# Moving the block-causal mask of the prompt attention from separate products into extra rows of its score products

## The chip, the cores and the metric

The kernel runs on one core of one Trainium2 chip. The metric is the device time of one execution in microseconds (us). Before the change the median of three executions is 3446.71 us (3445.31 to 3451.4).

## The reference

One inference step of a one-layer hybrid streaming encoder, in float32. What matters here is group A, attention with 8 heads over 2064 rows of a prompt (16 meta rows and 2048 frames) in chunks of 64 frames. A frame sees the meta rows and every frame of its own and of earlier chunks:

```python
chunk_p = jnp.where(frame_p < 0, -1, frame_p // CHUNK)          # CHUNK = 64

def attend(q, k, v, mask):
    s = jnp.einsum('bqhd,bkhd->bhqk', q, k).astype(jnp.float32) * (QK_HEAD ** -0.5)
    if mask is not None:
        s = jnp.where(mask, s, -jnp.inf)
    p = jax.nn.softmax(s, axis=-1).astype(v.dtype)
    return jnp.einsum('bhqk,bkhd->bqhd', p, v)

    # per block of queries: attend(q_blk, k, v, c_blk[:, None] >= chunk_id[None, :])
```

Queries and keys have 96 entries a head (64 without position, 32 with rotary position). Input projection, a gated delta rule (group B), the attention of 64 new rows over a cache, output projection and MLP are the rest of the work. The change leaves them alone.

## The kernel before

**Stages.** The program runs an input projection (0 to about 545 us), a gated delta rule with the queries' projection beside it (to about 975 us), the prompt's attention (about 977 to 1715 us), the attention of the new rows (to about 1810 us) and output projection with MLP (to the end). float32 products are taken as three products of a high and a low part.

**Attention.** A job is a head and a block of 512 queries: 4 pairs of heads, 2 heads, 4 blocks, 32 jobs in all, in an order written out in `HB0`. Keys lie in 17 tiles, mostly of 128, in 4 chunks that end where a block of 512 queries does. Three kinds of work are interleaved on the engines.

- `kv_chunk` works out keys and values of two heads for a chunk. The key tile `kn` holds rows of 97 numbers: 96 entries and a constant 1 in column 96, set by GpSimd (L866). TensorE transposes it (L913), and ScalarE and VectorE split it into the high part `KTh` and the low part `KTl`, with the key's entries in rows 0 to 96.
- `prep` makes a job ready. It loads the queries (L938, on SP's queue), and `q_head` transposes them (L925) and splits them into `qh` (L928, ScalarE) and `ql` (L929, VectorE). Then it finds the greatest score of each query: for each of the four groups of 128 queries a product over all keys that these see, in pieces of up to 512 keys (L952), and a maximum over each piece by VectorE (L955). On the last piece of each group a product with one row of contraction (L954) adds -1e30 to the last 64 keys for the first 64 queries. The four maxima a partition are transposed (L960), negated (L962) and sent by a DMA on SP's queue into row 96 of `qh` (L963), so that the product with the keys' constant 1 subtracts the maximum.
- `main_block` takes the transposed scores of a key tile as three products (L983, L984, L986) into PSUM, ScalarE takes their exponential (L990), ScalarE and VectorE split this in two (L133, L134), and four steps of work later three products with the values follow (L1003, L1004, L1005). The four key tiles that reach the diagonal get a fourth score product with two rows of contraction (L988), which adds -1e30 where a query does not see a key:

```python
edge = i > 4 * b
nc.tensor.matmul(ps[:w, off:], kl[:96, s:s + w], qh[:96, off:], start=False, stop=not edge)
if edge:
    nc.tensor.matmul(ps[:w, off:off + 128], self.negk[:, :w], self.negk[:, 128:], start=False, stop=True)
```

That makes 4 x 32 = 128 products on L954 and 128 on L988. Their operands are small constants that `attn_open` builds with VectorE.

**Order.** `attention` issues the units of the main blocks in order and, between them, as many steps of the two streams of side work (keys, preparation) as their deadlines call for; a preparation may begin three jobs ahead of its main block. Each engine and each DMA queue executes its list in a fixed order. `qh` and `ql` rotate over 4 buffers (`QB`), so the queries of job n take the buffer of job n-4. PSUM holds 2 score tiles, 3 tiles of the maxima's products, 1 of the results and 2 for the rest.

Of the kernel before, what the change touches and what calls it, by code (L numbers as in the profile page):

```python
# [22 lines left out]
T = LP + DEC  # L23
# [9 lines left out]
# columns of the transposed activations: new sample rows, meta rows, frames  # L33
# [29 lines left out]
# order of the output projection's products: group of columns, half of it, half of the rows  # L63
# [3 lines left out]
KVW, QW = 4, 8  # L67
PB, HB, SSB, QB = 5, 4, 2, 4
# [12 lines left out]
# key tiles of the prompt, in chunks that end where a block of 512 queries does  # L81
# [11 lines left out]
def key_chunk(c):  # L93
    """first column, columns and tiles of a chunk."""
    t = TILES[tile_index(c):4 * c + 5]
    return t[0][0], t[-1][0] + t[-1][1] - t[0][0], t


def prepass_cuts(b, i):
    """the keys that 128 queries see, in pieces (chunk, from, to)."""  # L100
    r = []
    for c in range(b + 1):
        s0, n, _ = key_chunk(c)
        n = min(n, 144 + 128 * (4 * b + i) - s0)
        k = -(-n // 512)
        r += [(c, n * j // k, n * (j + 1) // k) for j in range(k)]
    return r
# [10 lines left out]
class Prog:  # L118
# [17 lines left out]
    def rsqrt(self, out, v, tmp, eng=None):  # L136
        """out = v ** -0.5 for a tile v in SBUF; tmp: one scratch tile of the same shape."""
# [73 lines left out]
    def load_x(self, b):  # L211
        """a block of x^T in two parts and its reciprocal root mean squares."""
# [23 lines left out]
    def mean_rstd(self, ss, n, w, r=None):  # L236
        """[128, n] broadcast of (column sum of ss / w + eps) ** -0.5."""
# [23 lines left out]
    def col_product(self, w, b):  # L261
        """one tile of output columns of one block."""
# [25 lines left out]
    def finish_cols(self, batch, zs, b):  # L288
        """what needs several tiles of columns: the latents' norms; what TensorE waits for comes first."""
# [75 lines left out]
    def silu(self, y, z):  # L365
        """y = z * sigmoid(z), z kept."""
# [21 lines left out]
    def gdn_setup(self):  # L388
        """masks, then decays and betas of all chunks."""
# [47 lines left out]
    def gdn_prep(self, n, P):  # L437
        """what a chunk needs that does not depend on the state; a stage at a time."""
# [67 lines left out]
        # inverse of I + A, as T and U = T^T  # L506
# [35 lines left out]
        # one Newton step on the residual I - (I + A) T, A in two exact parts  # L542
# [87 lines left out]
    def phase_g(self, g=True, q=True, eb=None):  # L630
        """eb: where the pools of the attention's first keys stay open, which are worked out beside the last chunks."""
# [39 lines left out]
    def q_gen(self, c, ps_):  # L671
        """normalised and rotated queries, a stage at a time."""
# [51 lines left out]
    def rotate(self, p, key, x, tab, R, nt, nh):  # L724
        """rotate x [R, nt, nh, 32] in place, with gains."""
# [13 lines left out]
    def attn_early(self, es):  # L739
        """pools and constants of the first chunk of keys, open beside the end of the delta rule."""  # L740
# [7 lines left out]
        nc.sync.dma_start(self.kcs, I["rope_p"])  # L748
        self.lat, self.K, self.q = {}, {}, {}
# [9 lines left out]
    def attn_open(self, es):  # L759
        nc, I = self.nc, self.I  # L760
        c = self.pool(es, "b_const")
        self.bp = self.pool(es, "b")
        self.bps = self.pool(es, "b_ps", space=PSUM)
        neg = c.tile([1, 128], F32, name="neg")
        nc.vector.memset(neg, 0.0)
        nc.vector.memset(neg[:, 0:64], -1e30)
        self.negr = c.tile([1, 128], F32R, name="negr")
        nc.vector.tensor_copy(self.negr, neg)
        # an edge tile of 128 keys and 128 queries: the first half of the queries sees no key, the second the first 64
        neg2 = c.tile([2, 256], F32, name="neg2")  # L770
        nc.vector.memset(neg2[:, 0:128], -1e30)
        nc.vector.memset(neg2[:, 128:192], 1.0)
        nc.vector.memset(neg2[:, 192:256], 0.0)
        nc.vector.memset(neg2[0:1, 0:64], 0.0)
        nc.vector.memset(neg2[0:1, 128:192], 0.0)
        nc.vector.memset(neg2[0:1, 192:256], 1.0)
        self.negk = c.tile([2, 256], F32R, name="negk")
        nc.vector.tensor_copy(self.negk, neg2)
        self.oner = c.tile([1, 64], F32R, name="oner")
        nc.vector.tensor_copy(self.oner, self.ones[0:1, 0:64])  # L780

    def bt_(self, tag, bufs, shape=(128, 512), dt=F32):
        """a tile of a rotation of bufs, the first of which lie in the early pool."""
# [13 lines left out]
    def lat_chunk(self, c):  # L797
        """latents of a chunk of keys in two parts, its rotated keys and their sums of squares."""
# [53 lines left out]
    def kv_chunk(self, pair, c):  # L852
        """keys and values of two heads for a chunk of keys."""
# [7 lines left out]
        kn = self.bt_("kn", 2, (128, 5, 2, 97))[:, :nt]  # L861
# [4 lines left out]
        nc.gpsimd.memset(kn[:, :, :, 96:97], 1.0)  # L866
# [37 lines left out]
        for h in range(2):  # L904
# [3 lines left out]
            while i < nt:  # L908
                ps = self.bpsum("m")
                a = tiles[i][0] - s0  # L910
                while i < nt and tiles[i][0] - s0 + tiles[i][1] - a <= 512:
                    s, w = tiles[i]
                    nc.tensor.transpose(ps[:97, s - s0 - a:s - s0 - a + w], kn[:w, i, h, :], self.ident[:w, :w])  # L913
                    i += 1
                e = s - s0 + w
                self.split(kh[:97, a:e], kl[:97, a:e], ps[:97, :e - a])
# [3 lines left out]
    def q_head(self, q, h):  # L920
        """transposed queries of a head in two parts, rows 0..95."""
# [5 lines left out]
        lo = self.bt_("ql", QB, (128, 512), F32R)  # L927
        nc.scalar.activation(hi[:96], ps[:96], AF.Copy, scale=self.gqk[:96])  # L928
# [985 lines left out]
```

## Time and profile before

| what | value |
|---|---|
| median of 3 runs | 3446.71 us (3445.31 to 3451.4) |
| profiled execution, span | 3450.1 us |
| TensorE busy | 3328.1 us (96%), 20293 products |
| VectorE busy | 2705.7 us (78%) |
| ScalarE busy | 1585.4 us (46%) |
| GpSimd busy | 396.3 us (11%) |
| prompt attention, 977 to 1715 us | 738 us: TensorE busy 722.1, VectorE 531.8, ScalarE 493.4 |

The span is that of one profiled execution and lies inside the range of the runs. A busy time is the time in which an engine had an instruction under way. Products overlap one another and their ends are modelled, so the time that one takes from TensorE is read from where the next one starts, not from its own duration.

### The profile page before, as it was taken

What the parts mean: (1) busy time and instruction counts of PE and PEld (TensorE: products, weight loads), DVE (VectorE), ACT (ScalarE), POOL (GpSimd) and SP (SyncE); (2) the same over time, 40 slices, a digit from 0 to 9 for tenths busy, and PEclk for the clock granted to TensorE, in tenths of its full rate; (3) what the DMA queues carried; (4) which work ended last, traced back from release to release, by engine and by line L of the source; (5) the groups of instructions that cost most, each with busy time, mean ns of one, the idle gap of its engine ahead of it and who ended that gap; (6) DMA issues with size and microseconds to landing.
All of it is one profiled execution on the core that took longest, in us unless ns stands there. A gap on an engine that the chain in (4) does not pass through costs nothing.

```text
span 3450.1 us, 54900 instructions
## 1 busy us (share of the span) xinstructions
PE 3328.1 (96%) x20293; PEld 3018.3 (87%) x20293; DVE 2705.7 (78%) x5449; ACT 1585.4 (46%) x3495; POOL 396.3 (11%) x750
## 2 busy tenths in 40 slices
PE   9999998999879999999989999999999999999999
PEld 6888886888767777777679999999999999999999
DVE  7877555888857777777578888888988888988887
ACT  5555434555545757676655322233422233423222
POOL 0100014664410000000020100002100002100000
PEclk9999998999989999999999999999999999999999
DMA  4322113333111011100133222224222224222222
GB/s 130 86 74 71 62 71 101 91 111 82 44 53 28 13 33 25 26 21 25 31 109 100 76 74 74 74 74 155 88 71 71 72 75 143 72 73 76 73 73 70
DMA packets 317341, 247.48 MB, mean 72 GB/s; under 512 B 31328, under 2 KB 291152, under 8 KB 317008
## 3 DMA queue, kind: packets, MB, share of 16 engines
q1 hardware_dynamic: 299504, 218.56, 21.6%
q10 hardware_dynamic: 15536, 16.23, 1.6%
q0 software_dynamic: 2032, 9.18, 0.8%
q8 instruction: 159, 2.61, 0.3%
q14 instruction: 110, 0.90, 0.1%
HBM read 196.34 MB, written 47.50 MB: 71 GB/s over the span
## 4 chain that ended last, share of the span: by engine, by line
PE 74%; DVE 7%; ACT 2%; issue 2%; DMA 1%; POOL 1%; ACTq 0%; SPq 0%; POOLq 0%; DVEq 0%
PE psu L1593 23%; PE psd L1593 20%; PE pso L1005 3%; PE pso L1003 2%; PE pss L983 2%; PE pspre L952 2%; PE pso L1004 2%; PE pss L984 2%; PE pss L986 2%; PE ps L271 1%; PE ps L270 1%; PE ps L269 1%; PE pss L988 1%; PE pspre L954 1%; DVE lev L530 1%
## 5 line engine op out<-in xcount | busy, mean ns | idle before, releaser
L1593 PE MATMUL psu<-hh,uh 128*128 128x352 f32 x1728 | 563.2, 326 | 2.6 <-ACT uh L1489 2.1
L1593 PE MATMUL psu<-hl,uh 128*128 128x352 f32 x1728 | 557.6, 323 | 0.0
L1593 PE MATMUL psu<-hh,ul 128*128 128x352 f32 x1728 | 550.1, 323 | 0.0
L1593 PE MATMUL psd<-al,dh 128*128 128x352 f32 x1536 | 496.8, 324 | 3.3 <-DVE al L1782 3.3
L1593 PE MATMUL psd<-ah,dl 128*128 128x352 f32 x1536 | 495.3, 323 | 0.0
L1593 PE MATMUL psd<-ah,dh 128*128 128x352 f32 x1536 | 473.7, 324 | 11.1 <-DVE y L1701 7.3
L1701 DVE TENSOR_TENSOR y<-y,psd 128x352 f32<-128x352 f32 x768 | 386.8, 514 | 105.1 <-PE psd L1593 103.0
L1593 PEld LDWEIGHTS psu<-hh,uh 128*128 128x128 f32 x1728 | 326.0, 189 | 4.5 <-ACT uh L1489 2.5
L1593 PEld LDWEIGHTS psu<-hl,uh 128*128 128x128 f32 x1728 | 326.2, 189 | 1.2 <-issue 0.5
L269 PE MATMUL ps<-hhi,whi 128*128 128x512 f32 (+5 forms) x880 | 313.8, 360 | 11.3 <-ACT hhi L133 7.4
L1593 PEld LDWEIGHTS psu<-hh,ul 128*128 128x128 f32 x1728 | 324.0, 188 | 0.2 <-DVE ul L1467 0.2
L271 PE MATMUL ps<-hhi,wlo 128*128 128x512 f32 (+5 forms) x880 | 314.1, 358 | 0.2 <-DVE wlo L134 0.2
L270 PE MATMUL ps<-hlo,whi 128*128 128x512 f32 (+5 forms) x880 | 312.6, 356 | 0.1
L1593 PEld LDWEIGHTS psd<-ah,dh 128*128 128x128 f32 x1536 | 284.5, 188 | 16.8 <-DVE y L1701 11.4
L1593 PEld LDWEIGHTS psd<-al,dh 128*128 128x128 f32 x1536 | 289.6, 189 | 5.2 <-DVE al L1782 5.1
L1593 PEld LDWEIGHTS psd<-ah,dl 128*128 128x128 f32 x1536 | 289.4, 188 | 0.0
L1489 ACT CAST dh<-wr 128x512 fp32r<-128x512 f32 x192 | 119.2, 621 | 368.6 <-PE psd L1593 316.2
L1780 ACT CAST ah<-u 128x352 fp32r<-128x352 f32 x192 | 93.4, 486 | 396.9 <-DVE u L1778 279.1
L134 DVE TENSOR_TENSOR Pl<-P,Ph 128x512 fp32r<-128x512 f32 (+4 forms) x352 | 212.1, 612 | 71.3 <-ACT Ph L133 64.3
L990 ACT ACTIVATE P<-pss 128x512 f32<-128x512 f32 (+4 forms) x352 | 187.9, 539 | 150.6 <-PE pss L986 83.3
L955 DVE TENSOR_REDUCE mp<-pspre 128x1 f32<-128x296 f32 (+6 forms) x400 | 192.1, 502 | 80.3 <-PE pspre L952 65.8
L133 ACT CAST Ph<-P 128x512 fp32r<-128x512 f32 (+4 forms) x352 | 193.0, 561 | 10.3 <-PE pso L1004 2.6
(469 smaller groups left out, 7384.9 us busy)
## 6 DMA issues: line engine op xcount, KB each, us to landing
wr<-in_w_up SPq DMA_DIRECT2D x192, 256.0 KB
wr<-in_w_down SPq DMA_DIRECT2D x192, 256.0 KB
qn<-scr_qN SPq DMA_DIRECT2D x32, 384.0 KB
wr<-in_w_out SPq DMA_DIRECT2D x48, 256.0 KB
wraw<-in_w_in SPq DMA_DIRECT2D x42, 256.0 KB
scr_convT<-s SPq DMA_DIRECT2D x36, 256.0 KB
mixr<-scr_mixT SPq DMA_DIRECT2D x12, 704.0 KB
out_y_T<-y SPq DMA_DIRECT2D x48, 176.0 KB
```

Of the source, the lines that this page charges most:

```text
L133: nc.scalar.copy(hi, src)
L134: (lo_eng or nc.vector).tensor_tensor(lo, src, hi.bitcast(F32), op=ALU.subtract)
L269: nc.tensor.matmul(ps[:m, :n], whi[:, k, :m], hi[:, k], start=k == 0, stop=False)
L270: nc.tensor.matmul(ps[:m, :n], whi[:, k, :m], lo[:, k], start=False, stop=False)
L271: nc.tensor.matmul(ps[:m, :n], wlo[:, k, :m], hi[:, k], start=False, stop=k == 7)
L955: nc.vector.tensor_reduce(m[:, i:i + 1] if one else mp[:, j:j + 1], ps[:, :z - a], axis=AX.X, op=ALU.max)
L990: nc.scalar.activation(p[:w, off:], ps[:w, off:], AF.Exp)
L1005: nc.tensor.matmul(po[:, off:], v[:, 0:128], pl[:w, off:], start=False, stop=i == last)
L1489: self.nc.scalar.copy(t[0], src)
L1593: self.nc.tensor.matmul(ps, w, h, start=i == 0, stop=i == len(steps) - 1)
L1701: adds.append(nc.vector.tensor_tensor(Y[j][:, d], Y[j][:, d], ps, op=ALU.add).ins)
L1780: done = nc.scalar.copy(A[f, j][0], u).ins
```

## The change

The mask goes into the score products themselves. `kn` gets 8 more columns, so that the transposed keys have 105 rows (`KR`): row 96 is the constant 1, and the rows 97 to 104 say, for each of a chunk's last four key tiles j, that a key lies in tile j (row 97 + 2j) and that it lies in its second half (row 98 + 2j). The queries get rows 97 to 104 with -1e30: row 97 + 2j for the first 64 queries of group j, row 98 + 2j for its second 64. The products that need the mask contract over 105 rows, and the 256 mask products are gone. The keys' rows are copied by GpSimd from a constant in SBUF; the queries' rows (with a row 96 of zeros, which the maxima overwrite later) come by one DMA a job on SP's queue from a small array in DRAM.

```diff
+KR = 105
@@ attn_early
+        self.kmask = c.tile([128, 4, 2, KR - 96], F32, name="kmask")
+        self.first.dma_start(self.kmask, I["kmask"])
+        self.first.dma_start(self.S["qmask"], I["qmask"])
@@ attn_open
-        c = self.pool(es, "b_const")
-        neg = c.tile([1, 128], F32, name="neg")
...
-        self.oner = c.tile([1, 64], F32R, name="oner")
-        nc.vector.tensor_copy(self.oner, self.ones[0:1, 0:64])
@@ kv_chunk
-        kn = self.bt_("kn", 2, (128, 5, 2, 97))[:, :nt]
+        kn = self.bt_("kn", 2, (128, 5, 2, KR))[:, :nt]
...
-        nc.gpsimd.memset(kn[:, :, :, 96:97], 1.0)
+        if c == 0:
+            nc.gpsimd.memset(kn[:, 0, :, 97:], 0.0)
+            nc.gpsimd.memset(kn[:, 0, :, 96:97], 1.0)
+        nc.gpsimd.tensor_copy(kn[:, nt - 4:, :, 96:], self.kmask)
...
-                    nc.tensor.transpose(ps[:97, s - s0 - a:s - s0 - a + w], kn[:w, i, h, :], self.ident[:w, :w])
+                    nc.tensor.transpose(ps[:KR, s - s0 - a:s - s0 - a + w], kn[:w, i, h, :], self.ident[:w, :w])
...
-                self.split(kh[:97, a:e], kl[:97, a:e], ps[:97, :e - a])
+                self.split(kh[:KR, a:e], kl[:KR, a:e], ps[:KR, :e - a])
@@ q_head
         lo = self.bt_("ql", QB, (128, 512), F32R)
+        nc.sync.dma_start(hi[96:KR].bitcast(F32), self.S["qmask"])
         nc.scalar.activation(hi[:96], ps[:96], AF.Copy, scale=self.gqk[:96])
@@ prep
-                nc.tensor.matmul(ps[:, :z - a], qh[:96, i * 128:(i + 1) * 128], kh[:96, a:z], start=True, stop=not end)
-                if end:
-                    nc.tensor.matmul(ps[:, z - a - 64:z - a], self.negr, self.oner, start=False, stop=True)
+                r = KR if end else 96
+                nc.tensor.matmul(ps[:, :z - a], qh[:r, i * 128:(i + 1) * 128], kh[:r, a:z], start=True, stop=True)
@@ main_block
-                nc.tensor.matmul(ps[:w, off:], kh[:97, s:s + w], qh[:97, off:], start=True, stop=False)
+                r = KR if i > 4 * b else 97
+                nc.tensor.matmul(ps[:w, off:], kh[:r, s:s + w], qh[:r, off:], start=True, stop=False)
                 nc.tensor.matmul(ps[:w, off:], kh[:96, s:s + w], ql[:96, off:], start=False, stop=False)
-                edge = i > 4 * b
-                nc.tensor.matmul(ps[:w, off:], kl[:96, s:s + w], qh[:96, off:], start=False, stop=not edge)
-                if edge:
-                    nc.tensor.matmul(ps[:w, off:off + 128], self.negk[:, :w], self.negk[:, 128:], start=False, stop=True)
+                nc.tensor.matmul(ps[:w, off:], kl[:96, s:s + w], qh[:96, off:], start=False, stop=True)
@@ lay_out
+    km = np.zeros((128, 4, 2, KR - 96), np.float32)
+    km[:, :, :, 0] = 1.0
+    qm = np.zeros((KR - 96, 512), np.float32)
+    for j in range(4):
+        km[:, j, :, 1 + 2 * j] = 1.0
+        km[64:, j, :, 2 + 2 * j] = 1.0
+        for e in range(2):
+            qm[1 + 2 * j + e, 128 * j + 64 * e:128 * j + 64 * e + 64] = -1e30
```

The rest of the diff takes comments and docstrings out.

## Rows read from the trace of the kernel before

**Rows 1.** The page's first line.
```profile
span 3450.1 us, 54900 instructions
```
**Rows 2.** Busy us by engine in stretches: length, PE, PEld, DVE, ACT, POOL, clock.
```profile
977.00:1080.00 103.00, 90.01 (x403) 68.49 (x404) 70.81 (x196) 55.56 (x138) 5.92 (x16) 0.81 0.17 46
1080.00:1220.00 140.00, 139.72 (x692) 107.59 (x691) 103.91 (x254) 98.31 (x222) 2.25 (x8) 0.98 0.07 18
...
1250.00:1680.00 430.00, 429.62 (x2104) 328.40 (x2103) 319.37 (x756) 298.43 (x654) 3.28 (x12) 0.98 0.09 22
...
1297.00:1337.00 40.00, 40.00 (x224) 32.14 (x223) 34.22 (x85) 31.41 (x73) 1.00 (x4) 1.00 0.07 17
```
**Rows 3.** The chain that ended last, 960 to 1720 us, shares by line.
```profile
by line: PE pso L1005 11.9%; PE pso L1003 11.0%; PE pss L983 10.6%; PE pspre L952 10.5%; PE pso L1004 9.7%; PE pss L984 9.6%; PE pss L986 9.4%; PE pss L988 4.1%; PE pspre L954 3.7%; PE psm L913 2.1%; PE psm L925 2.0%; PE psm L879 2.0%; PE p
```
**Rows 4.** L954 alone: duration ns min/median/max, starts; idle before it.
```profile
L954 PE MATMUL pspre<-oner,negr x128: 292/292/418, 976.8 to 1669.7; 1*128 1x64 f32 x128
...
  issue: 21.8, 92
  DVE negr L768: 2.2, 2
```
**Rows 5.** L988 alone: the same.
```profile
L988 PE MATMUL pss<-negk x128: 267/322/472, 988.4 to 1713.1; 2*128 2x128 f32 x120, 2*64 2x128 f32 x8
...
  issue: 19.5, 64
```
**Rows 6.** L954's products, then L988's, in 977 to 1080: PE, PEld busy.
```profile
977.00:1080.00 103.00, 6.65 (x21) 4.38 (x21) 0.81 0.17 46
...
977.00:1080.00 103.00, 5.30 (x16) 3.00 (x16) 0.81 0.17 46
```
**Rows 7.** PE in order of time (start us, duration us): an edge tile, 512 columns.
```profile
1708.05 0.40 PE L984 MATMUL pss<-ql,KTh 96*128 96x512 f32 x1
1708.29 0.40 PE L986 MATMUL pss<-qh,KTl 96*128 96x512 f32 x1
1708.62 0.32 PE L988 MATMUL pss<-negk 2*128 2x128 f32 x1
1708.87 0.50 PE L1005 MATMUL pso<-Pl,V 128*128 128x512 f32 x1
```
**Rows 8.** PE, 1586 to 1588 us: an edge tile of 128 columns, a masked last piece.
```profile
1586.36 0.22 PE L983 MATMUL pss<-qh,KTh 97*128 97x128 f32 x1
1586.42 0.28 PE L984 MATMUL pss<-ql,KTh 96*128 96x128 f32 x1
1586.53 0.27 PE L986 MATMUL pss<-qh,KTl 96*128 96x128 f32 x1
1586.73 0.32 PE L988 MATMUL pss<-negk 2*128 2x128 f32 x1
1586.99 0.27 PE L960 MATMUL psm<-ident,m 128*4 128x128 f32 x1
...
1587.79 0.20 PE L952 MATMUL pspre<-KTh,qh 96*128 96x64 f32 x1
1587.92 0.29 PE L954 MATMUL pspre<-oner,negr 1*128 1x64 f32 x1
1588.14 0.50 PE L1005 MATMUL pso<-Pl,V 128*128 128x512 f32 x1
```
**Rows 9.** GpSimd's groups, 960 to 1715 us.
```profile
L831 POOL TENSOR_TENSOR kr<-kr,gk_bc 128x128 f32<-128x128 f32 x3 | 1.4, 480 | 18.7 <-ACT ksq L828 18.7
...
L866 POOL MEMSET kn<- 128x8 f32 x11 | 1.2, 113 | 368.3 <-PE psm L913 368.1
```
**Rows 10.** SP's queue, 960 to 1720 us: us waited, times, longest.
```profile
SPq L963 <- ACT mrow L962: 150.3, 12, 24.1
```
**Rows 11.** In order of time: a row of maxima sent, its reader on PE.
```profile
1230.12 0.60 SPq L963 DMA_DIRECT2D qh<-mrow  x1
...
1232.50 0.71 PE L983 MATMUL pss<-qh,KTh 97*80 97x512 f32 x1 [1.16 <-DMA qh<-mrow]
```
**Rows 12.** PE: job 27's last reader of `qh`; job 31's first L954 product.
```profile
1643.41 0.22 PE L986 MATMUL pss<-qh,KTl 96*64 96x128 f32 x1
...
1649.65 0.29 PE L954 MATMUL pspre<-oner,negr 1*128 1x64 f32 x1
```

More of the change, by code (lines that the diff above doesn't have):

```diff
@@ L759, in attn_open @@
     def attn_open(self, es):
-        nc, I = self.nc, self.I
-        c = self.pool(es, "b_const")
         self.bp = self.pool(es, "b")
         self.bps = self.pool(es, "b_ps", space=PSUM)
-        neg = c.tile([1, 128], F32, name="neg")
[L765 to L778, printed above, removed]
-        self.oner = c.tile([1, 64], F32R, name="oner")
-        nc.vector.tensor_copy(self.oner, self.ones[0:1, 0:64])
     def bt_(self, tag, bufs, shape=(128, 512), dt=F32):
@@ L1834 @@
 }
-SCRATCH = {"convT": (1536, T), "gateT": (512, T), "qlatT": (QL, T), "mixT": (1024, NQ), "qN": (17, 128, 768)}
+SCRATCH = {"convT": (1536, T), "gateT": (512, T), "qlatT": (QL, T), "mixT": (1024, NQ), "qN": (17, 128, 768), "qmask": (KR - 96, 512)}
 def lay_out(inp):
@@ L1889, in lay_out @@
     r["masks"] = c(np.stack(m, axis=1).astype(np.float32))
+    km = np.zeros((128, 4, 2, KR - 96), np.float32)
[6 more added lines that the diff above has]
+            qm[1 + 2 * j + e, 128 * j + 64 * e:128 * j + 64 * e + 64] = -1e30
+    r["kmask"], r["qmask"] = c(km), c(qm)
     return r
```

## The prediction

> **What bounds the kernel now.** Only the prompt's attention changes, so I read its stretches first, then the chain that ended last, then the mask products one by one. The stretches show TensorE (PE) without a pause from 1080 us on: 429.6 of 430 us between 1250 and 1680, while VectorE has 319.4 and ScalarE 298.4 [rows 2]. In the first stretch, 977 to 1080, PE is busy 90.0 of 103 us at a granted clock of 0.81, so part of it is at the lower of the two levels; there it is paced by others. A busy share can flatter PE, because its instructions overlap. The chain settles it: every line named in it is a PE line, and the two mask lines are in it with 4.1% and 3.7% [rows 3]. That is 7.8% of 760 us, 59 us, nearly all of what 256 products of about 0.23 us each would fill. The mask products lie on the path.
>
> **What one of them costs.** Their durations, 0.29 and 0.32 us [rows 4, 5], are not the price; starts are. On an edge tile of 512 columns L986 starts at 1708.29, L988 at 1708.62 and the next product at 1708.87 [rows 7]. From L986 to the product behind the mask that is 0.58 us, where an unmasked product of that width takes 0.24 (1708.05 to 1708.29). The mask costs 0.34. At 128 columns it is the same: 1586.53 to 1586.99 is 0.46, against 0.11 for the neighbour L984, a difference of 0.35 [rows 8]. So the price does not come from the columns. The idle time in front of the weight loads, put down to "issue" (21.8 us over 92 products and 19.5 over 64), says where it sits: these loads start late with no wait that the profile can name [rows 4, 5], and the product behind starts late as well. I take 0.34 for L988.
>
> For L954, the piece of 64 columns starts at 1587.79 and the product behind the mask at 1588.14: 0.35 us [rows 8]. Unmasked, such a short piece would take between 0.06 (L983 to L984) and 0.11 (L984 to L986), so the mask costs 0.24 to 0.29; before wider pieces the products of the edge tiles let me expect up to 0.34. I take 0.30, inside 0.24 to 0.34.
>
> A rule stands against this price. The Trainium skill, "TensorE: Matmul & The Clock Gate", section "Back-to-back issue gap", gives a product of up to 64 columns about 60 cycles and one of 128 columns 134 cycles at full clock, 25 and 56 ns. By that, 128 of each would cost 10.4 us in all, an estimate from that page; the starts above show six to twelve times as much for each.
>
> **The change, part by part.**
> - *Removed, 256 products.* 128 x 0.34 = 43.5 us and 128 x 0.30 = 38.4 us, 81.9 us of PE's time.
> - *What of it the path gives back.* 37 of the 256 lie in 977 to 1080 (21 and 16) [rows 6], worth 21 x 0.30 + 16 x 0.34 = 11.7 us; as PE is not the pace there I count half, 5.9. The other 219 are worth 70.2 us, where PE is. Does the next engine leave room? In 1250 to 1680 the masks make about 12% of PE's time at most, and VectorE's 319.4 us leave 110 us. In the tightest 40 us, 1297 to 1337, VectorE has 34.2 and ScalarE 31.4; a seventh of the time could go at most, and the share of the masks, 70.2 of the 635 us behind 1080, is 11%. The room is enough everywhere but not lavish, and engines that come close make each other wait; I take 0.9 of 70.2, 63.2 us. Together 69 us.
> - *Longer contractions.* L983 goes from 97 to 105 rows at edge tiles, L952 from 96 to 105 in last pieces. The step from 97 rows to 96 inside a tile (1586.36, 1586.42) costs what a step at equal rows would [rows 8], and columns are unchanged: 0, covered by nothing and needing nothing.
> - *Transposes and splits.* 136 transposes load 105 columns for 97; the kinds of one such load in this trace differ by well under 0.03 us, so 0 to 4 us; I take 1.
> - *GpSimd.* 16 memsets of 113 ns become 16 copies of 72 numbers a partition, which I bound by that and by the 480 ns of a copy-like operation of 128 [rows 9], plus two small memsets for each of the four first chunks: at most 16 x 0.48 + 8 x 0.11 = 8.6 us on an engine that waited 368 us in front of these very memsets. They run when the buffer comes free, long before the transposes that read it; cost 0. Without that cover it is at most 8.6 us.
> - *The queries' mask rows.* 32 more DMAs on SP's queue, 18 KB each, about 0.6 us to issue; the row of maxima is the nearest row, 2.4 us from issue (1230.12) to its reader on PE (1232.50) [rows 11]. New is a wait: the DMA needs the `qh` buffer that job n-4 has left, and the first masked product of a preparation needs the DMA. The tightest job is the last: its buffer's last reader starts at 1643.41 and its first L954 product at 1649.65 [rows 12], 6.2 us later, against 2.4. So 0, with up to 2 us for the first jobs, whose queries are split just ahead of their pieces; I take 1. Behind a waiting mask load on SP stand the next queries and rows of maxima; SP now waits 150.3 us for maxima anyway [rows 10], so it has nothing else to do.
> - *Constants.* VectorE's small operations in `attn_open` vanish, for which PE waited 2.2 us [rows 4]: a gain of 1 to 2. Two DMAs are added before the attention's first loads, about 1 us of SP's time, off the path. Together 1 us gained.
>
> Sum: 69 - 1 - 1 + 1 = 68 us. The profiled execution has a span of 3450.1 us [rows 1], 3.4 above the median of 3446.7; it becomes 3382, and the median, which I predict, 3446.7 - 68 = 3379 us. Late next is VectorE: in the tight 40 us it would have 34.2 of about 36.
>
> **The rivals.**
> - *Half is given back.* VectorE and ScalarE work at 70 to 85% in the same stretches, with few buffers in PSUM (2 score tiles, 3 of maxima). If PE then waits for exponentials and maxima at each edge, where tiles get small and per-instruction times weigh most, half of 81.9 comes back: 41 us, 3406. For it: the tight 40 us [rows 2]. Against it: the sums leave room in every stretch. Chance 0.13.
> - *Only the columns come back.* If the idle time around the masks would stay in another form, only the columns' time is won. A 64-column and a 128-column product at 0.06 to 0.11 us [rows 8] are 128 x 0.06 + 128 x 0.11 = 22 us: 3425. By the figures of the Trainium skill's page above ("TensorE: Matmul & The Clock Gate") it would be 10.4 us, 3436. Against: the gaps stand only around these two lines. Chance 0.04.
> - *More than forecast.* All of 81.9 us, and less time at the lower clock in the first stretch, where 0.81 means that about 40 of 103 us ran at 1.2 GHz; a quarter of the 20 us lost there is 5, with the constants' 2 and some slack 90: 3357. Chance 0.07.
> - *Slower, by SP's queue.* SP takes its list in a fixed order. If the mask load stands behind a row of maxima that is still being worked out, or parks the queue in front of one, PE, itself in order, stops at the first masked product. One landing for each of 32 jobs is 32 x 2.4 = 77 us, which would eat the gain; the kernel is slower from about 2.1 us a job on. If the rows of maxima are late too by as much, it is 154 us, and 3446.7 - 68 + 154 = 3533. For it: SP's long waits [rows 10] and the load's dependence on a buffer that comes free late. Against: 6.2 us at the tightest job [rows 12], and a lead of several steps (`QW`) between a job's transposes and its first piece. Chance 0.04.
> - *It doesn't do what it says.* A wait by whole buffer, say of `qh`'s split for the mask rows, could cost the 68 us at no one place: 0.02 for a time within 0.2%, which is about what a measurement of this kernel can tell from no change (7 us).
>
> **How the numbers follow.** The forecast has 0.70; its own range is 3365 to 3395 (0.8 to 1 of the 82 us, or prices of 0.24 and 0.31). The range 3355 to 3410 takes in the half and the larger gain. Faster is 0.70 + 0.13 + 0.04 + 0.07 = 0.94, the same 0.02, slower 0.04.
>
> **What would show it.** In the changed profile no product of one or two rows; 256 fewer on PE; L986's successor 0.24 us behind it at 512 columns on edge tiles; the attention's stage about 670 us for 738; VectorE's busy time unchanged in it but its share near 80%. A wait of the masked L952 products for the DMA of mask rows, above 10 us in all, would make the SP rival right; PE's waits for L990 and L955 growing by 30 us or more, the first rival; a stage above 735 us would make the prediction wrong altogether.

## The result, and the profile after the change

| | before | after |
|---|---|---|
| median of the runs shown with the result | 3449.06 us (3445.31 to 3454.07, 4 runs) | 3348.24 us (3346.45 to 3353.41, 4 runs) |
| profiled execution, span | 3450.1 us | 3344.6 us |
| attention, first L952/L944 product to last L1005/L993 product | 740.1 us | 651.0 us |
| from there to the new rows' input of the MLP (first `psu` product) | 95.3 us | 88.6 us |

The ratio is 0.9715, 95% interval 0.9695 to 0.9734: about 100 us faster, where 68 were forecast and 3355 was the low end. The direction and the place were right, the size was not. The rival "more than forecast" (3357) came nearest, and the result lies beyond it too.

Lines of the kernel after: the preparation's product is L944 (L952 before), its maximum L945 (L955), the scores L974, L975, L976 (L983, L984, L986), the exponential L978 (L990), the value products L991, L992, L993 (L1003, L1004, L1005), the row of maxima's DMA L953 (L963), the queries' mask rows L918, the keys' mask copy L856.

The page of the kernel after, its first line and its busy times:

```profile
span 3344.6 us, 54489 instructions
PE 3218.6 (96%) x20037; PEld 2963.2 (89%) x20037; DVE 2693.3 (81%) x5438; ACT 1577.2 (47%) x3495; POOL 400.9 (12%) x758
```

PE has 20293 - 20037 = 256 products fewer, as announced. Next, busy us by engine in two stretches, the attention and what follows it up to the first `psu` product (length, PE, PEld, DVE, ACT, POOL, granted clock, DMA share, GB/s); first before, then after:

```profile
974.77:1714.87 740.10, 723.28 (x3462) 551.43 (x3460) 533.66 (x1289) 494.02 (x1089) 11.45 (x36) 0.95 0.10 27
1714.87:1810.16 95.29, 80.50 (x501) 69.92 (x501) 71.83 (x157) 47.23 (x102) 21.15 (x41) 0.88 0.35 104
```
```profile
965.98:1617.00 651.02, 625.08 (x3205) 506.20 (x3204) 521.33 (x1278) 486.36 (x1089) 17.28 (x42) 0.95 0.12 31
1617.00:1705.56 88.56, 75.46 (x502) 65.80 (x501) 71.55 (x157) 46.93 (x102) 18.32 (x41) 0.96 0.37 109
```

The attention gave 89.1 us, the stretch behind it 6.7. PE still fills the attention (625 of 651 us) and VectorE stands at 521.33 / 651.02 = 80%, the share that was forecast, without having become the bound. In order of time (start, duration), an edge tile of the kernel after:

```profile
1589.27 0.40 PE L974 MATMUL pss<-qh,KTh 105*128 105x512 f32 x1
1589.51 0.40 PE L975 MATMUL pss<-ql,KTh 96*128 96x512 f32 x1
1589.74 0.40 PE L976 MATMUL pss<-qh,KTl 96*128 96x512 f32 x1
1589.97 0.34 PE L974 MATMUL pss<-qh,KTh 105*128 105x384 f32 x1
```

The successor of the third score product starts 0.23 us behind it; before it was 0.58 with the mask between [rows 7]. The product over 105 rows takes 0.24 and the ones over 96 take 0.23, as good as the same. The chain that ended last, 960 to 1620 us, by line:

```profile
by line: PE pss L974 11.6%; PE pso L991 11.4%; PE pss L975 11.0%; PE pso L993 10.9%; PE pss L976 10.8%; PE pso L992 10.6%; PE pspre L944 9.6%; DMA qh<-mrow 2.6%; PE psm L869 2.2%; PE psm L871 2.1%; PE psm L870 2.1%; PE psm L903 2.1%; PE psm
```

It is the chain of before [rows 3] without its two mask lines. What is late now is first the landing of the row of maxima (`DMA qh<-mrow`), with 2.6% or 17.0 us of the chain (5.6 before), and behind it VectorE's maxima (`mp`), with 10.4 us (4.2 before; the line above is cut off ahead of them).

### The profile page after: what moved, and what is told of

Its sections match the earlier page's. It is cut to its first block, busy times and chain, and to the rows that moved or that the text cites. A ratio compares the mean times of both kernels' runs of the same rounds, so it can differ in the third digit from the quotient of the medians.

```text
span 3344.6 us, 54489 instructions
## 1 busy us (share of the span) xinstructions
PE 3218.6 (96%) x20037; PEld 2963.2 (89%) x20037; DVE 2693.3 (81%) x5438; ACT 1577.2 (47%) x3495; POOL 400.9 (12%) x758
## 4 chain that ended last, share of the span: by engine, by line
PE 84%; DVE 8%; ACT 2%; issue 2%; DMA 2%; POOL 1%; ACTq 0%; SPq 0%; POOLq 0%; DVEq 0%
PE psu L1581 23%; PE psd L1581 21%; PE ps L270 5%; PE ps L271 5%; PE ps L272 5%; PE pss L974 2%; PE pso L991 2%; PE pss L975 2%; PE pso L993 2%; PE pss L976 2%; PE pso L992 2%; PE pspre L944 2%; DVE lev L531 1%; DMA qh<-mrow 1%; PE gpp L498 1%
## 5 line engine op out<-in xcount | busy, mean ns | idle before, releaser
L1581 PEld LDWEIGHTS psd<-ah,dh 128*128 128x128 f32 x1536 | 284.6, 188 | 16.7 <-DVE y L1689 11.4
L978 ACT ACTIVATE P<-pss 128x512 f32<-128x512 f32 (+4 forms) x352 | 185.9, 538 | 94.4 <-PE pss L976 85.6
L945 DVE TENSOR_REDUCE mp<-pspre 128x1 f32<-128x296 f32 (+6 forms) x400 | 189.1, 500 | 35.8 <-PE pspre L944 34.2
L1694 POOL TENSOR_TENSOR y<-y,v 128x352 f32<-128x352 f32 x40 | 40.3, 1030 | 1332.2 <-DVE y L1689 1332.1
```

Of the source, the lines that this page charges most:

```text
L945: nc.vector.tensor_reduce(m[:, i:i + 1] if one else mp[:, j:j + 1], ps[:, :z - a], axis=AX.X, op=ALU.max)
L978: nc.scalar.activation(p[:w, off:], ps[:w, off:], AF.Exp)
L1581: self.nc.tensor.matmul(ps, w, h, start=i == 0, stop=i == len(steps) - 1)
```

## The experiments

A sum of starts serves to compare the runs. Every product of the attention has a usual distance to the next start, the median for its line and columns at the full clock in the profiles that have no short products (after, e2, e5, e8). For the products that all kernels share, these distances add up to 571.6 us. What a distance has beyond the usual is lost, and is of one of three kinds: at the lower clock; at a mask product or one next to it; at any other product. 571.6 and the three make the length of the attention. A wait that happens to fall beside a mask counts as the mask's. Each run was timed next to runs of the kernel before on the same chip, and its ratio is against those; the three columns of losses, like the length of the attention, come from one profiled execution a run.

| run | median us (runs) | ratio, 95% interval | attention, us | lost at the masks | at other products | at the lower clock | stretch behind, us |
|---|---|---|---|---|---|---|---|
| before | 3449.06 (4) | | 740.1 | 106.6 | 14.8 | 47.1 | 95.3 |
| e1_before_again | 3444.83 (10) | 0.9989, 0.9969 to 1.0009 | 741.9 | 106.6 | 14.8 | 48.9 | 95.4 |
| after | 3348.24 (4) | 0.9715, 0.9695 to 0.9734 | 651.0 | 0 | 34.9 | 44.5 | 88.6 |
| e2_after_again | 3354.01 (4) | 0.9728, 0.9701 to 0.9756 | 650.7 | 0 | 35.0 | 44.2 | 89.2 |
| e3_main_only | 3413.57 (5) | 0.9916, 0.9886 to 0.9946 | 702.7 | 50.4 | 31.5 | 49.1 | 89.2 |
| e4_prep_only | 3402.62 (4) | 0.9878, 0.9848 to 0.9909 | 699.5 | 55.5 | 28.0 | 44.5 | 90.4 |
| e5_no_mask | 3362.06 (4) | 0.9759, 0.9731 to 0.9786 | 648.1 | 0 | 40.2 | 36.3 | 96.8 |
| e8_no_mask_again | 3355.87 (4) | 0.9737, 0.9712 to 0.9761 | 652.5 | 0 | 43.0 | 37.9 | 96.7 |
| e6_wide | 3363.19 (4) | 0.9769, 0.9737 to 0.9801 | 660.6 | 35.3 | 19.1 | 34.6 | 92.1 |
| e7_both | 3446.51 (10) | 1.0006, 0.9986 to 1.0026 | 746.1 | 104.2 | 19.7 | 50.5 | 90.8 |
| e9_rows64_32 | 3450.28 (1) | single run | 740.0 | 105.2 | 13.2 | 49.9 | 96.6 |
| e10_rows65_33 | 3396.95 (1) | single run | 685.8 | 70.7 | 16.8 | 26.7 | 97.9 |
| e11_wide_kn | 3427.25 (1) | single run | 729.7 | 104.8 | 15.1 | 38.2 | 93.0 |
| e12_wide_kn_again | 3446.12 (12) | 1.0003, 0.9980 to 1.0026 | 729.3 | 104.8 | 15.1 | 37.8 | 91.8 |

What one mask product costs, by the same usual distances: the median delay of the start behind it, and the further delay of the start after that, in us. In the main blocks of before the two together are 0.45 whether the product ahead has 512, 384 or 128 columns.

| kernel, rows in main blocks and preparation | main blocks: next start | one further | preparation: next start | one further |
|---|---|---|---|---|
| before, 2 and 1 | 0.345 | 0.104 | 0.315 | 0.103 |
| e9, 64 and 32 | 0.346 | 0.103 | 0.314 | 0.103 |
| e10, 65 and 33 | 0.064 | 0.051 | 0.316 | 0.102 |
| e6, 128 and 128 | 0.064 | 0.051 | 0.050 | 0.079 |

### One half of the change at a time

`e3_main_only` is the kernel after with the 128 short products of the preparation put back, `e4_prep_only` with those of the main blocks:

```diff
@@ e3_main_only, prep
-                r = KR if end else 96
-                nc.tensor.matmul(ps[:, :z - a], qh[:r, i * 128:(i + 1) * 128], kh[:r, a:z], start=True, stop=True)
+                nc.tensor.matmul(ps[:, :z - a], qh[:96, i * 128:(i + 1) * 128], kh[:96, a:z], start=True, stop=not end)
+                if end:
+                    nc.tensor.matmul(ps[:, z - a - 64:z - a], self.negr, self.oner, start=False, stop=True)
@@ e4_prep_only, main_block
-                r = KR if i > 4 * b else 97
-                nc.tensor.matmul(ps[:w, off:], kh[:r, s:s + w], qh[:r, off:], start=True, stop=False)
+                nc.tensor.matmul(ps[:w, off:], kh[:97, s:s + w], qh[:97, off:], start=True, stop=False)
...
+                if edge:
+                    nc.tensor.matmul(ps[:w, off:off + 128], self.negk[:, :w], self.negk[:, 128:], start=False, stop=True)
```

Not shown are the lines of `attn_open` that build the constants of these products again.

> The masks of the main blocks go into 105 rows, the 128 one-row products of the preparations stay. Theory A (each removed product gives back its whole price on TensorE, 0.34 to 0.37 us, and the time outside the attention moved by other causes): the attention's stage shrinks by 128 x 0.34 to 0.37, 44 to 47 us; whole time 3400 to 3407. Theory B (a part of the 100 us comes with the new rows, the loads and the order that the scheduler makes of them, not with the products): the same 44 to 47 us in the stage, and 12 to 16 us outside it in addition, 3386 to 3393. If PE's time were taken up by waits for the exponentials (the forecast's discount), 30 to 40 us.

> The masks of the preparations go into 105 rows, the 128 two-row products of the main blocks stay. Theory A: 128 x 0.30 to 0.35 us, 38 to 45 us less in the stage; whole time 3402 to 3411. Theory B: 12 to 16 us outside the stage in addition, 3388 to 3397. Together with the run before this one: by theory A the two gains add to the gain of the whole change in the stage (89 us), by theory B the gain outside would be counted twice.

Busy times of the attention, e3 and then e4:

```profile
973.39:1676.09 702.70, 674.81 (x3333) 531.01 (x3332) 529.85 (x1282) 494.11 (x1089) 17.62 (x42) 0.94 0.11 29
```
```profile
974.12:1673.65 699.53, 678.24 (x3333) 528.03 (x3332) 527.39 (x1285) 494.46 (x1089) 17.97 (x42) 0.95 0.11 29
```

Without the main blocks' short products (e3) 56.2 us less is lost at the masks (106.6 - 50.4), without the preparation's (e4) 51.1. Of that 16.7 and 13.2 come back as losses at other products (14.8 to 31.5 and to 28.0), so that each half alone keeps 38 to 40 us. The half that goes second is worth more, 47 and 49 us, since the losses elsewhere then grow by 3.4 and 6.9 only. That is why the attention gains 37.4 and 40.6 us by the halves and 89.1 by both. So theory A missed e3, by some 7 us in the attention, and the halves do not add up to the whole; the 30 to 40 us of the last case are what e3 gave. e4's 40.6 lie inside what theory A said. Theory B's 12 to 16 us outside the attention came in neither run: the stretch behind it is 5 to 6 us shorter.

### The mask left out, and the mask kept but as tall as its neighbours

`e5_no_mask` is the kernel before without the 256 products and without anything in their place: the mask isn't applied, and the scores are scaled by a further 0.02, so that the exponentials stay finite:

```diff
@@ e5_no_mask, prep
...
-                if end:
-                    nc.tensor.matmul(ps[:, z - a - 64:z - a], self.negr, self.oner, start=False, stop=True)
@@ main_block
...
-                if edge:
-                    nc.tensor.matmul(ps[:w, off:off + 128], self.negk[:, :w], self.negk[:, 128:], start=False, stop=True)
@@ attn_early
-        nc.vector.tensor_scalar(self.gqk, self.gqk, float(np.float32(QKH ** -0.5)), None, op0=ALU.mult)
+        nc.vector.tensor_scalar(self.gqk, self.gqk, float(np.float32(0.02 * QKH ** -0.5)), None, op0=ALU.mult)
```

`e6_wide` is the kernel before with all 256 products, whose constants are filled up with zeros to 128 rows:

```diff
@@ e6_wide, attn_open
-        neg = c.tile([1, 128], F32, name="neg")
+        neg = c.tile([128, 128], F32, name="neg")
...
-        neg2 = c.tile([2, 256], F32, name="neg2")
+        neg2 = c.tile([128, 256], F32, name="neg2")
+        nc.vector.memset(neg2, 0.0)
...
-        self.oner = c.tile([1, 64], F32R, name="oner")
-        nc.vector.tensor_copy(self.oner, self.ones[0:1, 0:64])
+        self.oner = c.tile([128, 64], F32R, name="oner")
+        nc.vector.tensor_copy(self.oner, self.ones[:, 0:64])
```

> The kernel before without its 256 mask products and with nothing in their place: the mask is left out, and the scores are scaled down by 50 so that the exponentials stay finite. Theory A: the time of the changed kernel within 5 us (3343 to 3353), as the added rows, copies and loads cost nothing on the path. Theory B: 12 to 16 us more than the changed kernel (3360 to 3365), as the order outside the attention stays that of before. If the loads of mask rows cost something in the changed kernel, this one is faster than it: under 3340.

> The kernel before with all 256 mask products kept, but contracting over 128 rows, the added ones zero. If what makes them dear is the short contraction (one or two rows between products of 96 and more), each falls from about 0.35 to the 0.06 to 0.11 us of an ordinary product as narrow, and 256 x 0.24 to 0.29 us come back: 61 to 74 us, 3375 to 3388. If a small product behind a large one is dear however many rows it has (its issue, or the writing to the same bank), nothing changes: 3445 to 3453.

The attention of e6, and in order of time one of its edge tiles:

```profile
967.19:1627.79 660.60, 641.41 (x3462) 528.91 (x3460) 524.85 (x1289) 489.38 (x1089) 11.41 (x36) 0.96 0.11 30
```
```profile
1622.48 0.40 PE L986 MATMUL pss<-qh,KTl 96*128 96x512 f32 x1
1622.72 0.23 PE L988 MATMUL pss<-negk 128*128 128x128 f32 x1
1622.78 0.44 PE L1005 MATMUL pso<-Pl,V 128*128 128x512 f32 x1
```

e6 has the 3462 products of before, on the same columns, and 79.5 us less in the attention. Of that 71.3 us are at the masks (106.6 - 35.3), inside the 61 to 74 that were expected; 12.5 are at the lower clock, which no run ties to the products, and 4.3 came back at other products. The product behind the mask starts 0.06 us after it, where it took 0.25 with two rows [rows 7], and the mask itself no longer starts late. So two thirds of what 256 products cost was neither their number nor their columns: it was how few rows they contract. The other 35.3 us stay as long as the products are there.

The kernel after is no dearer than no mask at all: without what is lost at the lower clock its attention has 606.5 us, those of e5 and e8 611.8 and 614.6. The medians fit that only in part: e5 came out 14 us above the kernel after, as theory B had it, but e8, on the same chip as e2 below, 2 us above (3355.87 and 3354.01), as theory A had it. The added rows, copies and loads of the change cost nothing that these profiles show.

### Before and after again, with the short products put back on top

> The kernel before, unchanged, for a second profile. Theory A: what lies outside the attention varies from run to run by several us without any change (delta rule 428 to 437 us, new rows 88 to 97 us in the profiles so far, in step with the time at the lower granted clock), so this profile may differ from the first by as much, and the attention's stage is 740 us within 5. Theory B (the changed kernel's gain outside the attention comes from its lists): the delta rule 434 us and the new rows 95 us again, within 2.

> The changed kernel, unchanged, for a second profile and more runs. Theory A: delta rule and new rows anywhere in 428 to 437 and 88 to 97 us, the stage 651 us within 5, median 3348 to 3360. Theory B: delta rule 428, new rows 89 us again, within 2, and the median stays at 3348 within 4, clear below the kernel without masks (3362).

`e7_both` is the kernel after with the 256 short products added again, so that the mask is applied twice; `e8_no_mask_again` is e5 once more, on the chip of e2. The constants are built again as in e3 and e4.

```diff
@@ e7_both, prep
-                nc.tensor.matmul(ps[:, :z - a], qh[:r, i * 128:(i + 1) * 128], kh[:r, a:z], start=True, stop=True)
+                nc.tensor.matmul(ps[:, :z - a], qh[:r, i * 128:(i + 1) * 128], kh[:r, a:z], start=True, stop=not end)
+                if end:
+                    nc.tensor.matmul(ps[:, z - a - 64:z - a], self.negr, self.oner, start=False, stop=True)
@@ main_block
...
+                if edge:
+                    nc.tensor.matmul(ps[:w, off:off + 128], self.negk[:, :w], self.negk[:, 128:], start=False, stop=True)
```

> The changed kernel with all 256 short mask products put back on top: the mask is applied twice. The difference to the changed kernel is the price of the products in the new setting, the difference to the kernel before that of the added rows, copies and loads. Theory A: the time of before within 5 us, 3443 to 3453, stage 740 us. Theory B: 12 to 16 us less, about 3434, with the gain outside the stage. If the loads of mask rows cost something on the path that the removed products hid: over 3455.

> The kernel without any mask once more (the mask is left out and the scores are scaled down), on the same chip as the changed kernel. Theory A: within 5 us of the changed kernel's median there, stage 648 us. Theory B: 10 us or more above it, with delta rule about 437 and new rows about 96 us as in its first profile.

The attention of e7, then that of e2:

```profile
968.41:1714.50 746.09, 728.62 (x3461) 554.88 (x3460) 532.94 (x1289) 495.44 (x1089) 18.35 (x42) 0.94 0.10 27
```
```profile
970.99:1621.74 650.75, 624.95 (x3206) 505.67 (x3204) 521.27 (x1278) 486.25 (x1089) 17.29 (x42) 0.95 0.12 31
```

The short products cost 746.1 - 650.9 = 95 us of the attention, and the kernel is back at the time of before (1.0006): what the change removed makes the whole effect, as far as the interval of this ratio tells (5 us less to 9 us more). What the change added is not without a trace in e7. Its attention is 4 to 6 us longer than those of before and e1, mostly by 4.9 us more at other products, and the stretch behind it 4.5 us shorter; the two cancel in the total. At the masks 104.2 us are lost again, and the losses elsewhere fall from 34.9 to 19.7. So a part of the waits that the kernel after shows lies hidden behind the masks, or is counted with them, when these are there. e1 and e2 repeat the attention of before and after within 2 us and below 1.

### At how many rows the price goes away

`e9_rows64_32` and `e10_rows65_33` are e6 with fewer of the 128 rows used: 64 in the main blocks and 32 in the preparation, then 65 and 33.

```diff
@@ e9_rows64_32
-                    nc.tensor.matmul(ps[:, z - a - 64:z - a], self.negr, self.oner, start=False, stop=True)
+                    nc.tensor.matmul(ps[:, z - a - 64:z - a], self.negr[:32], self.oner[:32], start=False, stop=True)
...
-                    nc.tensor.matmul(ps[:w, off:off + 128], self.negk[:, :w], self.negk[:, 128:], start=False, stop=True)
+                    nc.tensor.matmul(ps[:w, off:off + 128], self.negk[:64, :w], self.negk[:64, 128:], start=False, stop=True)
```

> The kernel before with its 256 mask products kept, those of the main blocks contracting over 64 rows, those of the preparations over 32 (the added rows zero). If a product pays whenever its contraction falls into a smaller class of rows than its neighbours' (Trainium skill, TensorEngine Tiling: modes of 32, 64 and 128 rows, a change of mode drains the engine), 64 and 32 rows are as dear as 2 and 1: stage 740 us within 6, total 3440 to 3455. If the price falls off with more rows, the stage is between 661 and 735.

> The same with 65 rows in the main blocks and 33 in the preparations. By the classes of 32, 64 and 128 rows the main blocks' products are free of the price from 65 rows on (they share the class of 96 to 128) and the preparations' (33, class of 64) are not: the stage falls by about 128 x 0.3, to 700 us within 6, and an edge tile of 512 columns has its successor within 0.40 us of L986 where it was 0.58. If one row more makes no such step, the stage is that of the run with 64 and 32 rows.

An edge tile and the attention of e9, then of e10 with a masked last piece of its preparation:

```profile
1659.18 0.40 PE L986 MATMUL pss<-qh,KTl 96*128 96x512 f32 x1
1659.51 0.33 PE L988 MATMUL pss<-negk 64*128 64x128 f32 x1
1659.76 0.50 PE L1003 MATMUL pso<-Ph,V 128*128 128x512 f32 x1
1660.10 0.40 PE L1004 MATMUL pso<-Ph,V 128*64 128x512 f32 x1
```
```profile
971.07:1711.06 739.99, 724.23 (x3461) 552.21 (x3460) 533.97 (x1289) 493.27 (x1089) 11.57 (x36) 0.95 0.10 27
```
```profile
1587.54 0.25 PE L952 MATMUL pspre<-KTh,qh 96*128 96x192 f32 x1
1587.72 0.29 PE L954 MATMUL pspre<-oner,negr 33*128 33x64 f32 x1
1587.95 0.50 PE L1003 MATMUL pso<-Ph,V 128*128 128x512 f32 x1
...
1655.41 0.40 PE L986 MATMUL pss<-qh,KTl 96*128 96x512 f32 x1
1655.65 0.23 PE L988 MATMUL pss<-negk 65*128 65x128 f32 x1
1655.71 0.45 PE L1005 MATMUL pso<-Pl,V 128*128 128x512 f32 x1
1655.99 0.39 PE L1003 MATMUL pso<-Ph,V 128*128 128x512 f32 x1
```
```profile
974.94:1660.72 685.78, 670.07 (x3461) 532.79 (x3460) 529.60 (x1289) 491.31 (x1089) 12.30 (x36) 0.97 0.11 29
```

From L986 to the product behind the mask it is 0.58 us with 64 rows, as with two, and 0.30 with 65; the one after starts 0.34 and 0.28 behind that, where 0.23 is usual. At the counts that were run the price is a step, not a slope: 0.45 in all at 2 and at 64 rows, 0.12 at 65 and at 128. The preparation's product with 33 rows still pays 0.42 in full. Of the 55 us that e10's attention is shorter, 34 to 36 are at the masks and 20 to 22 at the lower clock. The first part is what was expected of the products; because of the second the attention, at 685.8 us, came out below the 694 to 706 that were expected. Whether the products had a part in the second is not shown: this is one execution.

The Trainium skill, "TensorEngine Tiling (Array Packing)", sections "Available Configurations" and "Key Properties", knows modes in which TensorE works on tiles of 128, 64 or 32 rows, and says that changing the mode drains the engine. A step between 64 and 65 rows, a late start both of the mask and of the product behind it, and a price that does not depend on columns all agree with it. That a product of 64 rows or fewer changes such a mode by itself is my reading: the trace names no mode.

### Whether places in SBUF had a part in it

The wider key tile of the change moves other tiles. `e11_wide_kn` is the kernel before with that tile 105 wide and 97 of it used; `e12_wide_kn_again` is the same kernel, with twelve runs.

```diff
-        kn = self.bt_("kn", 2, (128, 5, 2, 97))[:, :nt]
+        kn = self.bt_("kn", 2, (128, 5, 2, 105))[:, :nt, :, :97]
```

> The kernel before with tiles of 105 numbers a row for the keys of which 97 are used as before: nothing but the places of buffers in SBUF changes. If the 6 us that the new rows' stage gains in all kernels with 105 rows come from where its buffers lie (its first load behind VectorE's last result instead of behind the DMA of the last output), that stage takes 88 to 92 us here and the attention 740 within 5. If they come from the rows, loads or products, it stays at 95 to 97.

> The kernel before with nothing but a wider tile: the keys' tile has 105 columns allocated and 97 used, so the instructions and their order are those of before and only places in SBUF differ. One look gave 3427.25 us beside 3458.37 for before on the same chip, with an attention stage of 729.7 us for 740. Theory 'places matter for this kernel': the ratio to before stays at 0.990 to 0.996 (15 to 35 us faster), and the stage stays at 728 to 733 us; then a part of what the change won could come from the places that its wider tile moved. Theory 'chance of one look, by the granted clock': ratio 0.998 to 1.002 with an interval that holds 1, stage 737 to 744 us, and nothing of the 100 us belongs to places. Most likely to me is the second, since a kernel with the extra rows and the 256 short products put back came out at 1.0006.

The attention of e11 and of e12:

```profile
962.90:1692.56 729.66, 714.61 (x3461) 544.95 (x3460) 532.68 (x1289) 493.21 (x1089) 11.47 (x36) 0.96 0.10 27
```
```profile
973.93:1703.26 729.33, 714.67 (x3461) 544.99 (x3460) 532.98 (x1289) 493.59 (x1089) 11.49 (x36) 0.96 0.10 27
```

The single run of e11 (3427 beside 3458) was misleading: twelve runs of e12 gave 1.0003. The two profiles do agree on an attention ten us shorter, and the table says what it is: 38 us lost at the lower clock for 47 and 49, with the other losses as before. Why the clock fell for less time in both profiles, when the median shows none of it, stays open; what is lost at the masks is not touched by it. The stretch behind the attention took 93.0 and 91.8 us in these two profiles, between what was expected with and without a part of the places in it.

## Why the prediction was wrong in its size

**Place and mechanism: right.** The 256 products lay on the path, their price sat in late starts and not in columns, and it went away with them. That the price hangs on the rows of contraction was not in the prediction; e6, e9 and e10 showed it. The 10.4 us that the prediction made from the table of gaps (the Trainium skill, "TensorE: Matmul & The Clock Gate", section "Back-to-back issue gap") are of isolated products, and the same section says that such gaps under-count small products in a stream of weight loads and products. The table does not hold for products of 1 to 64 rows here; for a mask product of 128 columns and 128 rows its 56 ns are near the 64 ns by which the next start moves in e6.

**The failed step: "What one of them costs", 81.9 us.** The price was read from the product ahead of the mask to the product behind it, and there it was about right: 0.34 was taken for L988, 0.345 is the median; 0.30 for L954, 0.315 is the median. But the next start is late as well. In order of time, the two products that follow the edge tile of before in [rows 7], whose last start is 1708.87:

```profile
1709.21 0.40 PE L1003 MATMUL pso<-Ph,V 128*128 128x512 f32 x1
1709.44 0.39 PE L1004 MATMUL pso<-Ph,V 128*64 128x512 f32 x1
```

1708.87 to 1709.21 is 0.34, where 0.23 is usual, as in the next step. These 0.10 us stand behind nearly every mask (the medians of the table) and were not counted: 256 x 0.104 = 27 us. The price is 128 x 0.449 + 128 x 0.418 = 111 us, for 81.9: this term was too small by 29 us. The trace of before had it, one line below the last that was read.

**"What of it the path gives back": right in kind, wrong in place.** 0.84 of the price was to be kept (69 of 81.9). With the lower clock left out the attention became 86.5 us shorter, 0.78 of 111. In equal times of 103 us from the first product of the preparation, the value products L1005 before and L993 after (length, PE with its products, PEld, clock, DMA share, GB/s):

```profile
974.77:1077.77 103.00, 12.04 (x28) 5.88 (x28) 0.81 0.15 42
```
```profile
965.98:1068.98 103.00, 13.95 (x35) 7.27 (x35) 0.84 0.19 51
```

35 for 28. The 24th starts 89.9 us into the attention before and 75.8 after: 14 us, where 35 masks lay ahead of it, worth 15 by the full price; between e1 and e2 it is 13. So the first stretch kept most of it, where half was credited; its clock of 0.81 was no sign that PE doesn't set the pace there. What was not gained was lost behind it: 89.1 - 14 = 75 us for the other 221 masks, whose price is 96, so 0.78 where 0.9 was taken. The waits of PE and of its weight loads (us in total, times, longest) say where; first before, then after:

```profile
PEld pspre L954 <- issue: 21.8, 92, 0.4
PEld pss L988 <- issue: 19.5, 64, 0.4
...
PE pss L983 <- DMA qh<-mrow: 2.6, 3, 1.2
...
PEld pspre L952 <- DVE mp L955: 2.4, 8, 0.5
...
PEld pss L983 <- DMA qh<-mrow: 2.0, 2, 1.5
```
```profile
PEld pss L974 <- DMA qh<-mrow: 11.0, 9, 2.6
...
PE pss L974 <- DMA qh<-mrow: 8.8, 9, 2.3
...
PEld pspre L944 <- DVE mp L945: 5.7, 16, 0.9
```

The 41 us of late loads without a cause are gone. The row of maxima is late nine times for three, the maxima 16 times for 8. Before, the longest wait for that row stood between 1220 and 1250 us, where PE was busy 27.8 of 30 us; the prediction's "without a pause from 1080 us on" passed over it. By the product that starts late, the 20 us that came back at other products are 5 at the maxima's products (L944), 4 at the first score products (L974), 5 at the value products L991 and L992, and the rest spread over the others. Together that is like the first rival's mechanism, at a fifth of the price and not at half; its mark, 30 us more in the waits for L990 and L955, was not reached. The forecast named VectorE as late next; the landing of the maxima's row and what delays the value products have as large a part.

**The small terms.** Longer contractions at 0 were right: a first score product of 512 columns takes 0.235 us to the next start over 105 rows as over 97. The two starts that the prediction read for it [rows 8] do not show this, as they are 0.06 and 0.11 us apart. GpSimd's copies at 0 were right too:

```profile
L856 POOL COPY kn<-kmask 128x72 f32<-128x72 f32 x13 | 6.2, 478 | 315.1 <-PE psm L903 117.0 <-ACT P L978 100.4 <-ACT KTh L134 75.5
```

A copy takes 478 ns, the top of the bound, but GpSimd waited 315 us in front of them. The rival "slower, by SP's queue" is refuted. What SP took to issue each of the 32 mask rows (ns, least, median, most):

```profile
L918 SPq DMA_DIRECT2D qh<-scr_qmask x32: 265/289/503, 766.0 to 1555.9; - x32
```

No product is listed as waiting for them; 0.29 us each is half of what was put down.

**What the sum left out.** There are two smaller gains outside the products. The attention loses 44.5 and 44.2 us at the lower clock for 47.1 and 48.9, 3 to 5 us less; that is not clear of chance, since e11 and e12, with the instructions of before, lost 38. And the stretch behind it, which the prediction did not look at, is 6 to 7 us shorter. It lasts 88.6 to 90.8 us in the five profiles of kernels with mask rows and 91.8 to 97.9 in the others; less half of its time at the lower clock (21.9 us before, 6.8 after) it lasts 84 to 87 in all fourteen, so the difference is one of the clock. Its first two times 20 us, before and then after:

```profile
1715.00:1735.00 20.00, 10.66 (x35) 6.57 (x33) 8.52 (x15) 9.07 (x15) 2.87 (x6) 0.71 0.51 136
1735.00:1755.00 20.00, 20.00 (x94) 16.94 (x94) 15.49 (x21) 12.68 (x24) 10.36 (x15) 0.78 0.43 126
```
```profile
1617.00:1637.00 20.00, 13.33 (x66) 9.66 (x66) 11.62 (x18) 11.36 (x18) 6.25 (x8) 0.83 0.53 148
1637.00:1657.00 20.00, 19.02 (x107) 15.77 (x106) 16.45 (x25) 14.11 (x29) 7.09 (x21) 1.00 0.37 110
```

Before, PE worked 10.7 of the first 20 us and then ran at 0.78; after, it worked 13.3 and ran at full clock. SP's wait in front of its first load there (`kr_s`), in us, times and longest, before and then after:

```profile
SPq L1178 <- DMA scr_mixT<-u: 10.5, 1, 10.5
```
```profile
SPq L1166 <- DVE r L1008: 9.6, 1, 9.6
```

Before, the load waits for the landing of the attention's last output and starts at 1723.81, 8.9 us after the last value product; after, it waits for VectorE and starts at 1621.41, 4.4 us after it. The five kernels with mask rows all wait for VectorE there and the nine others for the landing. What in the change brings this about is open. That a tile which moved in SBUF lets the load start earlier is not shown, and the key tile alone does not do it: e11 and e12 moved it and kept the wait for the landing.

**The account.** 68 forecast, plus 29 on the price, less 12 because more of it was not gained (25 us for 13), plus 1 for small terms that were not to be seen, is the 86 of the attention; 3 to 5 of clock in it and 6 to 7 behind it make 95 to 98. The interval of the ratio holds 92 to 105 us (0.0266 and 0.0305 of 3449). The remaining stages don't tell more: against before they gave 9.8 us in the one pair of profiles and took 8.2 in the other. The upper end of the prediction's own range does not follow from its terms either: 0.8 of the 82 us ends at 3381, not at 3395.

## What to carry to other kernels

A product that contracts few rows among products that contract many is priced by its row count, not by its columns: 0.42 to 0.45 us here at 1, 2, 32, 33 and 64 rows. Put it into free rows of a neighbouring product, as this change does, or fill its operands with zeros to the neighbours' height, which alone gave a ratio of 0.977 here for a few edited lines (its profile also lost 12 us less at the lower clock). And read such a price from starts, on past the next product, until the distances are the usual ones again; then ask what waits were hidden behind it, for these come out (here a fifth of the price).

## What the runs showed of the hardware that was not expected

- The step at 64 rows: a mask product in the main blocks delays what follows by 0.45 us with 64 rows and by 0.12 with 65.
- A price can sit in two starts: the product behind a short one is late, and the one after that by another 0.10 us.
- Kernels with the same instructions differ by the granted clock: the attention of before had 76.2 and 81.5 us at the lower level, e11 and e12 had 56.6 and 56.3. The delta rule ahead of it, whose products no kernel here changes, lasted 426.3 to 437.1 us (from its first product, `gpp`, to the attention), and executions of the kernel before ran from 3426 to 3461 us. A single run could not have told effects of under 20 us.
